# Hybrid decoder block, fp32: the mixer's temporaries move from one pool before the split buffers to two pools around them, and its block orders are searched anew

## Chip, core and metric

One NeuronCore of one Trainium2 chip runs the whole block. The metric is device time in microseconds (us) per execution; the time of a kernel is the median of its runs. Profiled executions are described by a span (first to last instruction), which is a little shorter than the device time of the same execution.

## What is computed

The reference is one decoder layer on 256 tokens of width 2048, in float32, with D_FF = 5632:

```python
x = x + 0.5 * swiglu_ffn(rms_norm(x, ffn1_norm), ffn1_w_gate, ffn1_w_up, ffn1_w_down)
z = rms_norm(x, mix_norm) @ w_in                  # 2048 x 5120: lru_x, lru_gate, sc_b, sc_c, sc_x
xc = causal_depthwise_conv(lru_x, lru_conv_w) + lru_conv_b
h = rg_lru(xc, lru_w_a, lru_b_a, lru_w_i, lru_b_i, lru_lambda)
y_lru = h * gelu(lru_gate)
y_sc = sc_b * causal_depthwise_conv(sc_c * sc_x, sc_conv_w)
y = concatenate([rms_norm(y_lru, lru_out_norm), rms_norm(y_sc, sc_out_norm)])
x = x + y @ w_out                                 # 2048 x 2048
x = x + 0.5 * swiglu_ffn(rms_norm(x, ffn2_norm), ffn2_w_gate, ffn2_w_up, ffn2_w_down)
out = rms_norm(x, final_norm)
```

## The kernel before

**Arithmetic.** TensorE (PE) multiplies in fp32r, which keeps fewer bits than float32. Every operand is therefore kept as two fp32r tiles: `hi`, the value rounded, and `lo`, the rest. A weight tile arrives by DMA as `raw` (128 x 4 x 512 f32, 1 MB), ScalarE (ACT) casts it to `hi` in two halves (CAST 128x1024), VectorE (DVE) subtracts (`lo = raw - hi`, TENSOR_TENSOR 128x2048), and PE forms hi*hi, hi*lo and lo*hi. A set of such a weight tile is called a unit. In a PE row `out<-a,b`, a is the moving operand (512 columns, or 256) and b the stationary one (128 columns). In most blocks the weights move; in the plain blocks `in_x` and `in_b` the weights are stationary and the normalised input `xT_nm` moves.

**Blocks.** Large products are done in blocks by a seven-product scheme in the manner of Strassen and Winograd (`sevens`, line 542): units `p0` to `p6` are seven products of weight quarters or of their sums (12 matmuls of 512 columns each), and units such as `x00` or `x11` are ordinary products for the rest of the inner dimension (24 matmuls each). ACT and DVE put the results together in PSUM and in temporaries. An order such as `"c": ["-", "p0", "p4", "x01", ...]` says in which order PE does the units of a block; `X0`, `X1`, `g2`, `g3` are short fillers: two sets of transposes of the product of conv inputs (`pt_c`), and gate matmuls (`pgate`).

**Stages.** FFN1 runs to about 694 us; the mixer (`mix`, line 1713) to about 945 us: plain block `in_x` (x of the LRU), blocks `c`, `x`, `g` (each a call of `sevens`), plain block `in_b`, and the first output column `o0`; then `lead` (line 2326): output column `o3`, the block `o_q`, and the start of FFN2, which runs to the end.

**The order of work** is not decided at run time. `Plan` (line 57) is a list scheduler in the kernel's own source: each step has an engine, a length, needs, and perhaps a list of `rooms` (buffers) of which it takes the one that comes free first, by the plan's own clock. The steps are written out in the order that it finds, so each engine's queue is a fixed list. SyncE (SP) issues the loads in order, and an issue that waits for its buffer holds up all later ones. A wait that the plan didn't foresee is still honoured: the tile framework puts a semaphore wait on any instruction whose bytes are still in use by an earlier one.

**Memory.** Two stacks of pools lie in SBUF (left and right). From the left: constants, ten big blocks (B0 to B9, `bigs`), then in the FFN stages a pool of 11 temporaries of 2048 bytes per partition (22,528 bytes), and behind it three pairs of split buffers, `pair0` to `pair2` (hi 8192 and lo 8192 bytes each); from the right: raw buffers `raw0` to `raw4` and a spare. Layout "three" of `open_stage` (line 331) has three pairs and five raws, layout "two", for the mixer, two pairs and three raws. In the mixer the pool of temporaries, "mix", is 11 tiles `m` of 4160 bytes (4 x 259 f32, since some hold 3 columns of convolution history, rounded up) and 6 tiles `k` of 2048 bytes: 58,048 bytes ahead of the pairs. So pair0 begins at byte 112,224 of a partition in the FFN stages and at byte 147,744 in the mixer; pair1 begins at 128,608 and at 164,128; hi and lo are 8192 bytes apart. Divided by 128 the first of each leaves 96, the second 32; the big blocks leave 96. In blocks x and g the units take pair0, pair1 and a pair of big blocks (B4, B5) in turn (`thirds`); block c, o0 and the plain blocks use the two pairs alone. FFN1's pair2 lies at bytes 144,992 to 161,376, raw3 and raw4 from 165,792 to 182,176.

**Between stages**, `hand_over` (line 368) tells the next plan when each buffer comes free, from the offsets of pairs and raws in the two layouts, both counted from the start of pair0. `lead` starts its plan with it.

The places that the change and the prediction touch: `Place` (line 1670), `mix_orders` (1705), `middle`, `small`, `keep`, `large_one` in `mix` (1713 on), and the first lines of `lead` (2326). Rows of the profile all carry line 42, the helper that records every operation; they are told apart by tile names.

Of the kernel before, what the change touches and what calls it, by code (L numbers as in the profile page):

```python
# [10 lines left out]
F32 = mybir.dt.float32  # L11
F32R = mybir.dt.float32r
# [4 lines left out]
P = 128  # L17
D = 2048
S = 256
# [3 lines left out]
CW = 512  # L23
NC_D = D // CW
UK = 4
NH = 8
# [174 lines left out]
def hybrid_block(ctx: ExitStack, tc: tile.TileContext, a: dict, out: bass.AP):  # L201
# [4 lines left out]
    x = a["x"][0]  # L206
# [3 lines left out]
    bigs = ctx.enter_context(tc.tile_pool(name="bigs", bufs=10, side="left"))  # L210
# [15 lines left out]
    def f32(ap):  # L226
        return ap.bitcast(F32)
# [103 lines left out]
    def open_stage(layout, raws=None):  # L331

        n = len(opened) + 1
        left, right = layouts[layout]
        for side, names in (("left", left), ("right", right)):
            for name in names:
                pools[name] = pool_of(f"{name}_{n}", side, 2 if name == "spare" else 1)
        if raws:
            recent["raw"] = deque(raws)
        recent["pair"] = deque([i for i in recent["pair"] if i < len(left)] + [i for i in range(len(left)) if i not in recent["pair"]])  # L340
        opened.append(layout)
# [11 lines left out]
    for layout, (left, right) in layouts.items():  # L353
        sizes = dict(short0=6, short1=6, tall1=10, tall2=10, kept0=10, kept1=10, spare=4)
        at, span = 0, {}
# [5 lines left out]
        at = 92.375  # L361
# [6 lines left out]
    def hand_over(ready, old, new):  # L368

        out = {}  # L370
        for name, (lo, hi) in spans[new].items():
            times = [ready.get(n, Plan.EARLY) for n, (a, b) in spans[old].items() if a < hi and lo < b]
            out[name] = max(times, default=Plan.EARLY)
        return out
# [153 lines left out]
    def fetch(plan, w, cs, runs, name, rooms):  # L528
        got = {}

        def run(room):
            rows = sum(n for _, n in runs)
            raw = got["raw"] = pools[room].tile([P, rows, CW], F32, tag="raw", name=f"raw_{name}")
            at = 0
            for k, n in runs:
                sp.dma_start(raw[:, at : at + n, :], w[k * P : (k + n) * P, cs].rearrange("(j p) c -> p j c", p=P))
                at += n

        step = plan.load(sum(n for _, n in runs), run, rooms)
        return step, lambda: got["raw"]  # L540
# [407 lines left out]
    def whole(u):  # L948
        return [(UK * u, UK)]

    def quad(tile):
        return tile.rearrange("p (j c) -> p j c", j=UK)
# [692 lines left out]
    n1 = Norm("n1", vec["ffn1_norm"])  # L1645
# [23 lines left out]
    def past_steps(plan, old, steps):  # L1669
        at = max([z.end for z in steps if z.end is not None], default=Plan.EARLY) - old.free["PE"]  # L1670
        return [plan.add("", 0.0, None, *[z for z in steps if z.end is None], at=at)]

    class Place:
# [3 lines left out]

        def first(self, plan, engine, length, fn, *needs, **more):
            def run(room):
                self.tile = self.make()  # L1680
                fn()

            self.owner = plan.add(engine, length, run, *needs, room=self.rooms, **more)
            return self.owner
# [6 lines left out]
        def keep(self):  # L1691
            self.owner.readers.append(Step("", 0.0, None, (), 0.0, None, Plan.EARLY))
# [7 lines left out]
    for name in blocks_of:  # L1700
# [2 lines left out]
    tt_256, tt_512, tt_1024, ts_256 = 0.35, 0.6, 1.17, 0.41  # L1703
    act_256, act_512, act_1024, scaled_256, scaled_512 = 0.33, 0.6, 1.05, 0.43, 0.67
    mix_orders = {
# [4 lines left out]
    }  # L1710
    rs, yT, kept_yv = [], [], []
# [1 line left out]
    def mix(old):  # L1713
        free, ready = old.finish()
        end = old.free["PE"]
        mixer = ExitStack()
        room = mixer.enter_context(tc.tile_pool(name="mix", bufs=1, side="left", reuse_waits="tile"))
        open_stage("two")
        mixer.callback(close_stage)
        plan = Plan(free, hand_over(ready, "three", "two"))  # L1720
        plan.take(old)
        plan.table, plan.patience = "sqrt", 1.0
        raws, mids, smalls = [f"raw{i}" for i in range(3)], [f"m{i}" for i in range(11)], [f"k{i}" for i in range(6)]
        large = [f"B{i}" for i in range(6)]
        thirds = iter([0, 1, "x"] * 20)
        pairs = iter([0, 1] * 60)

        past = lambda steps: past_steps(plan, old, steps)

        def middle(name, w=S, dt=F32, rooms=None):  # L1730
            return Place(rooms or mids, lambda: room.tile([P, UK, w], dt, tag="m", name=name, bufs=len(mids)))

        def small(name):
            return Place(smalls, lambda: room.tile([P, CW], F32, tag="k", name=name, bufs=len(smalls)))

        def keep(name):
            return room.tile([P, CW], F32, tag="k", name=name, bufs=len(smalls))

        def large_one(name, dt=F32R, rooms=None):
            return Place(rooms or large, lambda: bigs.tile([P, UK, 2 * S], dt, tag="big", name=name))  # L1740

        turned = {c: [] for c in range(NC_D)}
        for c in (0, 1):
# [19 lines left out]

        si = Stationaries()
        xis = [large_one(f"xis_{i}", rooms=[f"B{i}"]) for i in range(2)]
        spare = small("spare_i")
        quads = {(t, u): lambda t=t, u=u: nm.exact[:, :, u * S + t * P : u * S + (t + 1) * P] for t in range(NT) for u in range(2)}

        def part_of(i):
            o = S * (i in (5, 2))  # L1770
            x = xis[0 if i in (4, 5) else 1].tile
            return x[:, :, o : o + P], x[:, :, o + P : o + S]

        def operand_sums():
            def spare_quad():
                return quad(spare.tile)

            exact = {(t, u): past(held["turned", u][1]) for t in range(NT) for u in range(2)}
            fills, steps = sums_in_steps(
                plan, si, lambda: nm.xT[0], lambda: nm.xT[1], quads, spare_quad,  # L1780
                {i: (lambda i=i: part_of(i)[0], lambda i=i: part_of(i)[1]) for i in (4, 5, 6, 2)}, exact,
            )
            for place, step in ((spare, steps[0]), (xis[0], fills[4][0]), (xis[1], fills[6][0])):
                place.owner = step
                step.room = place.rooms

                def run(room, place=place, fn=step.fn):
                    place.tile = place.make()
                    fn()

                step.fn = run
            fills[5][0].needs.append(fills[4][0])
            fills[2][0].needs.append(fills[6][0])
            spare.owner.readers += steps
            for x in xis:
                x.keep()
            xv = Step("", 0.0, None, (), 0.0, None, Plan.EARLY)
            xv.readers = list(steps)
            plan.tenant["B5"] = xv
            return fills  # L1800
# [73 lines left out]
        def gate_weights(key, src, place):  # L1874
            got = {}

            def run(room):
                got["raw"] = pools[room].tile([P, NH, P], F32, tag="raw", name=f"rawgate_{key}")
                sp.dma_start(got["raw"], src.rearrange("h i j -> i h j"))

            load = plan.load(2, run, raws)
            both = Place([place], lambda: bigs.tile([P, 2, NH, P], F32R, tag="big", name=f"gate_{key}"))
            wgate[key] = both
            hi = both.first(plan, "ACT", act_1024, lambda: act.copy(both.tile[:, 0], got["raw"]), load)
            lo = both.by(
                plan, "DVE", tt_1024, lambda: dve.tensor_tensor(both.tile[:, 1], got["raw"], f32(both.tile[:, 0]), op=ALU.subtract), hi
            )
            load.readers += [hi, lo]
            gates_known.extend([hi, lo])
# [395 lines left out]
        for g in range(2):  # L2285
# [7 lines left out]
            for k in (2 * g, 2 * g + 1):  # L2293
                load, raw = fetch(plan, w_out, slice(0, CW), whole(k), f"o0_{k}", raws)
# [13 lines left out]
            class Factor:  # L2308
                name = f"y{g}"

            rs.append(Factor())
            known = factor_in_steps(plan, rs[g], [a], n=D // 2, source=lambda got=got: got["ps"][:, :NT], due=6.0)
# [13 lines left out]
    def lead(keep):  # L2326
        old, added, exact = held["mixed"]
        free, ready = old.finish()
        plan = Plan(free, hand_over(ready, "two", "three"))
        plan.patience = 1.0  # L2330
        plan.take(old)
        rooms = [f"raw{i}" for i in range(5)]
# [16 lines left out]
                home["spare"] = quad(keep("yspare"))  # L2349
            return home["spare"]  # L2350

        known = past_steps(plan, old, exact)
        fills, _ = sums_in_steps(
            plan, so, lambda: yT[0].tile, lambda: yT[1].tile, {(t, u): y(t, u) for t in range(NT) for u in range(2)}, spare,
            {i: (lambda i=i: sum_part(i)[0], lambda i=i: sum_part(i)[1]) for i in (4, 5, 6, 2)},
# [20 lines left out]
        for g in range(2):  # L2376
# [7 lines left out]
            for k in (2 * g, 2 * g + 1):  # L2384
                load, raw = fetch(plan, w_out, slice(3 * CW, 4 * CW), whole(k), f"o3_{k}", rooms)
# [31 lines left out]
        return plan, turned, turn, pairs, [last]  # L2417

    held["mixed"] = mix(held["left"])

    fss = const.tile([P, NT, NC_D], F32, name="fss")
# [165 lines left out]
```

## Time and profile before

| | |
|---|---|
| median of 3 runs | 1708.87 us (1708.69 to 1709.17) |
| profiled execution, its own time | 1708.86 us |
| its span | 1707.1 us |
| mean granted TensorE clock | 0.997 |
| instructions | 20060 |
| HBM read | 339.82 MB, 200 GB/s over the span |

A row of the timeline reads: start, length, engine, line, operation, tiles, shape, count, and in brackets the idle time just before it with what ended it. Matmuls overlap by some 0.16 us at their ends, so the difference of two starts, not the length, tells a group's rate. A row of the chain gives start, length and work on the path that ended last, where "SPq" is SyncE issuing and "DMA" a transfer. The table of windows has for each stretch the busy time of each engine, the granted clock and the DMA share.

### The profile page before, as it was taken

How to read it: one execution, taken by the hardware profiler on the slowest of the kernel's cores; microseconds unless marked ns; L12 is line 12 of the kernel's file. 1: busy time of each engine (PE TensorE's matmuls, PEld its weight loads, DVE VectorE, ACT ScalarE, POOL GpSimd, SP SyncE). 2: the span in 40 equal slices, each digit the busy share in tenths (PEclk: the TensorE clock that was granted, in tenths of full speed). 3: DMA queues.
4: the chain of work that ended last, by engine and by line, in shares of the span. 5: the costliest groups of instructions: out<-in, count | busy, mean ns of one | idle time of the engine just before them, and what ended most of it. 6: DMA issues, size and time to landing. Idle time of an engine off the chain costs nothing.

```text
span 1707.1 us, 20060 instructions
## 1 busy us (share of the span) xinstructions
PE 1691.3 (99%) x7733; PEld 1402.9 (82%) x7733; DVE 1549.7 (91%) x1271; ACT 1117.5 (65%) x1303; POOL 68.3 (4%) x90
## 2 busy tenths in 40 slices
PE   9999999999999999999999999999999999999998
PEld 7888888888888888887888788888888888888886
DVE  7999899999899999798899778999899998999997
ACT  6775576666566668587786575665666665667665
POOL 0200000000000000000000000000000000000000
PEclk9999999999999999999999999999999999999999
DMA  8777877768777968487854786777768878868884
GB/s 283 225 258 211 280 230 237 256 187 262 253 258 228 292 180 266 149 264 223 269 170 135 246 255 196 254 244 211 246 188 264 269 222 246 278 217 249 247 249 145
DMA packets 185295, 398.79 MB, mean 234 GB/s; under 512 B 8052, under 2 KB 10992, under 8 KB 178928
## 3 DMA queue, kind: packets, MB, share of 16 engines
q1 hardware_dynamic: 174912, 340.81, 57.0%
q0 software_dynamic: 10112, 55.65, 16.8%
q8 instruction: 60, 0.98, 0.2%
q10 hardware_dynamic: 176, 1.06, 0.2%
q14 instruction: 35, 0.29, 0.0%
HBM read 339.82 MB, written 2.10 MB: 200 GB/s over the span
## 4 chain that ended last, share of the span: by engine, by line
PE 98%; DMA 1%; ACT 1%; DVE 0%; SPq 0%; issue 0%; DVEq 0%; ACTq 0%
PE ps_u_a L42 10%; PE ps_g_a L42 10%; PE ps_d_a L42 9%; PE ps_u_c L42 6%; PE ps_g_c L42 6%; PE ps_d_c L42 5%; PE ps_u_d L42 4%; PE ps_g_d L42 4%; PE ps_d_d L42 4%; PE ps_d_e L42 4%; PE ps_d L42 4%; PE ps_g_e L42 3%; PE ps_in_x L42 3%; PE ps_in_b L42 3%; PE ps_u L42 2%; PE ps_u_e L42 2%
## 5 line engine op out<-in xcount | busy, mean ns | idle before, releaser
L42 ACT CAST hi_g_p<-raw_g_w 128x1024 fp32r<-128x1024 f32 (+1 forms) x140 | 172.6, 1263 | 114.1 <-DVE raw_g_w L42 42.9
L42 ACT CAST hi_u_p<-raw_u_w 128x1024 fp32r<-128x1024 f32 (+1 forms) x140 | 172.5, 1262 | 93.3 <-PE ps_u_a L42 37.5
L42 DVE TENSOR_TENSOR lo_g_p<-raw_g_w,hi_g_p 128x2560 fp32r<-128x2560 f32 (+2 forms) x90 | 199.4, 2228 | 29.9 <-PE ps_d L42 11.4
L42 DVE TENSOR_TENSOR lo_u_p<-raw_u_w,hi_u_p 128x2560 fp32r<-128x2560 f32 (+2 forms) x90 | 199.5, 2229 | 14.7 <-ACT hi_u_p L42 12.4
L42 ACT CAST hi_d_p<-raw_d_w 128x1024 fp32r<-128x1024 f32 x140 | 141.2, 1047 | 78.7 <-DVE raw_d_w L42 39.6
L42 DVE TENSOR_TENSOR lo_d_p<-raw_d_w,hi_d_p 128x2048 fp32r<-128x2048 f32 (+1 forms) x90 | 162.5, 1814 | 11.2 <-ACT hi_d_p L42 9.8
L42 ACT CAST hi_d_x<-raw_d_x 128x1024 fp32r<-128x1024 f32 x72 | 73.2, 1046 | 36.0 <-PE ps_d_c L42 11.9
L42 DVE TENSOR_TENSOR lo_d_x<-raw_d_x,hi_d_x 128x2048 fp32r<-128x2048 f32 x36 | 82.2, 2286 | 6.7 <-ACT hi_d_x L42 6.6
L42 DVE TENSOR_TENSOR raw_g_w<-raw_g_w,raw_g_w 128x1024 f32<-128x1024 f32 (+2 forms) x50 | 86.5, 1755 | 1.4 <-DMA raw_g_w<-in_ffn_w_gate_dram 0.9
L42 DVE TENSOR_TENSOR raw_u_w<-raw_u_w,raw_u_w 128x1024 f32<-128x1024 f32 (+2 forms) x50 | 86.7, 1756 | 0.6
L42 ACT CAST hi_g_x<-raw_g_x 128x1536 fp32r<-128x1536 f32 x40 | 59.1, 1478 | 24.2 <-DMA raw_g_x<-in_ffn_w_gate_dram 16.5
L42 DVE TENSOR_TENSOR lo_u_x<-raw_u_x,hi_u_x 128x1536 fp32r<-128x1536 f32 x40 | 70.1, 1752 | 1.1 <-ACT hi_u_x L42 1.0
L42 DVE TENSOR_TENSOR lo_g_x<-raw_g_x,hi_g_x 128x1536 fp32r<-128x1536 f32 x40 | 70.1, 1752 | 0.4 <-ACT hi_g_x L42 0.4
L42 ACT CAST hi_u_x<-raw_u_x 128x1536 fp32r<-128x1536 f32 x40 | 59.0, 1476 | 15.8 <-DMA raw_u_x<-in_ffn_w_up_dram 8.6
L42 PE MATMUL ps_u_a<-hi_u_p,xT_n 128*128 128x512 f32 x240 | 61.1, 390 | 0.0
L42 PE MATMUL ps_g_a<-hi_g_p,xT_n 128*128 128x512 f32 x240 | 60.9, 389 | 0.0
L42 PEld LDWEIGHTS ps_g_a<-hi_g_p,xT_n 128*128 128x128 f32 x240 | 45.1, 188 | 9.3
L42 PEld LDWEIGHTS ps_u_a<-hi_u_p,xT_n 128*128 128x128 f32 x240 | 44.9, 188 | 9.2
L42 DVE TENSOR_TENSOR raw_d_w<-raw_d_w,raw_d_w 128x1024 f32<-128x1024 f32 x40 | 48.2, 1220 | 0.3
L42 PE MATMUL ps_d<-hi_d,h 128*128 128x512 f32 x192 | 45.7, 390 | 0.0
L42 PEld LDWEIGHTS ps_d<-hi_d,h 128*128 128x128 f32 x192 | 35.9, 188 | 7.4
L42 PE MATMUL ps_d_a<-hi_d_p,h 128*128 128x512 f32 x160 | 40.0, 392 | 0.0
(581 smaller groups left out, 4159.1 us busy)
## 6 DMA issues: line engine op xcount, KB each, us to landing
raw_g_w<-in_ffn_w_gate_dram SPq DMA_DIRECT2D x40, 1024.0 KB, 6.4
raw_u_w<-in_ffn_w_up_dram SPq DMA_DIRECT2D x40, 1024.0 KB, 6.2
raw_d_w<-in_ffn_w_down_dram SPq DMA_DIRECT2D x40, 1024.0 KB, 6.0
raw_d_x<-in_ffn_w_down_dram SPq DMA_DIRECT2D x36, 1024.0 KB, 6.3
raw_g_x<-in_ffn_w_gate_dram SPq DMA_DIRECT2D x40, 768.0 KB, 7.6
raw_u_x<-in_ffn_w_up_dram SPq DMA_DIRECT2D x40, 768.0 KB, 7.0
raw_d_w<-raw_d_w POOLq DMA_DIRECT2D x20, 1024.0 KB, 7.4
raw_d<-in_ffn_w_down_dram SPq DMA_DIRECT2D x12, 1024.0 KB, 8.2
```

What stands on the lines that cost most here:

```text
L42: ins = getattr(self.engine, name)(*args, **kwargs)
```

## The change

The pool "mix" is replaced by two. "near" stands where "mix" stood and holds 2 tiles `n` of 4096 bytes and 7 tiles `k` of 2048 bytes: 22,528 bytes, the same as the feed-forwards' pool of temporaries, so that pair0 and pair1 begin at bytes 112,224 and 128,608 in the mixer too. "far" stands behind the two pairs, from byte 144,992 on: 4 tiles `mp` of 4160 bytes, which alone can hold the convolution's history, and 5 tiles `m` of 4096. There are 11 tiles of the middle size as before, and 7 small ones where there were 6. The orders of blocks c, x and g are new. In `lead`, the buffers hi2, lo2, raw3 and raw4, which lie where "far" lies, are held not to be free before the last of the `m` and `mp` tiles; and one list of steps also waits, in the plan alone, for the last of `n` and `k`. The counts of instructions on each engine stay the same; apart from blocks c, x and g, each engine's order stays the same too, though what its instructions wait for does not.

```diff
     mix_orders = {
-        "c": ["-", "p0", "p4", "x01", "p5", "p2", "p6", "x11", "p3", "p1", "x00", "x10", "g2", "g3"],
-        "x": ["-", "p0", "p1", "p4", "x01", "p2", "p5", "x11", "p6", "x00", "p3", "x10"],
-        "g": ["-", "p0", "p4", "X1", "x11", "x01", "p5", "p1", "p6", "p2", "x00", "x10", "p3", "X0"],
+        "c": ["-", "p0", "p4", "x01", "p5", "p1", "p6", "x11", "p2", "p3", "x00", "x10", "g3", "g2"],
+        "x": ["-", "p0", "p1", "p4", "x01", "p5", "p2", "p6", "x11", "x00", "p3", "x10"],
+        "g": ["-", "p0", "p4", "X0", "x01", "p5", "p1", "X1", "x11", "p6", "p2", "p3", "x10", "x00"],
...
-        room = mixer.enter_context(tc.tile_pool(name="mix", bufs=1, side="left", reuse_waits="tile"))
+        near = mixer.enter_context(tc.tile_pool(name="near", bufs=1, side="left", reuse_waits="tile"))
         open_stage("two")
         mixer.callback(close_stage)
+        far = mixer.enter_context(tc.tile_pool(name="far", bufs=1, side="left", reuse_waits="tile"))
...
-        raws, mids, smalls = [f"raw{i}" for i in range(3)], [f"m{i}" for i in range(11)], [f"k{i}" for i in range(6)]
+        raws, mids, smalls = [f"raw{i}" for i in range(3)], [f"mp{i}" for i in range(4)], [f"k{i}" for i in range(7)]
+        plain = ["n0", "n1"] + [f"m{i}" for i in range(5)] + mids
...
-        def middle(name, w=S, dt=F32, rooms=None):
-            return Place(rooms or mids, lambda: room.tile([P, UK, w], dt, tag="m", name=name, bufs=len(mids)))
+        def middle(name, w=S, dt=F32):
+            def make(room):
+                if room[0] == "n":
+                    return near.tile([P, UK, w], dt, tag="n", name=name, bufs=2)
+                tag = room.rstrip("0123456789")
+                return far.tile([P, UK, w], dt, tag=tag, name=name, bufs=len(mids) if tag == "mp" else 5)
+
+            return Place(plain if w == S else mids, make)
...
     def lead(keep):
         old, added, exact = held["mixed"]
         free, ready = old.finish()
-        plan = Plan(free, hand_over(ready, "two", "three"))
+        after = hand_over(ready, "two", "three")
+        for name in ("hi2", "lo2", "raw3", "raw4"):
+            after[name] = max(t for n, t in ready.items() if n[0] == "m")
+        plan = Plan(free, after)
...
-        known = past_steps(plan, old, exact)
+        exact = past_steps(plan, old, exact)
+        known = [plan.add("", 0.0, None, *exact, at=max(t for n, t in ready.items() if n[0] in "kn"))]
```

What the change moves is shown at three places. First, SyncE's queue at the end of the mixer, where the loads of `o3` (the first work of `lead`) follow those of `o0`. Numbers at the ends of names count tiles; what stands in brackets are the semaphores that an issue waits for, by engine or DMA queue. Before:

```order
L42 DMA raw_o0_2_7254<-in_w_out_dram 128x4x512 [waits DMAHW0_49,DVE_49]
L42 DMA raw_o0_3_7300<-in_w_out_dram 128x4x512 [waits DMAHW1_49,DVE_49]
L42 DMA raw_o3_0_7515<-in_w_out_dram 128x4x512 [waits DVE_49,PE_49]
L42 DMA raw_o3_1_7517<-in_w_out_dram 128x4x512
L42 DMA raw_o3_2_7519<-in_w_out_dram 128x4x512 [waits DMAHW2_49]
L42 DMA raw_o3_3_7521<-in_w_out_dram 128x4x512 [waits DMAHW3_49]
L42 DMA raw_o_q_w11_7525<-in_w_out_dram 128x4x512 [waits DMAHW4_49,DVE_49]
```

And now:

```order
L42 DMA raw_o0_2_7252<-in_w_out_dram 128x4x512 [waits DMAHW0_49,DVE_49]
L42 DMA raw_o0_3_7317<-in_w_out_dram 128x4x512 [waits DMAHW1_49,DVE_49]
L42 DMA raw_o3_0_7519<-in_w_out_dram 128x4x512 [waits DMAHW2_49,DVE_49]
L42 DMA raw_o3_1_7521<-in_w_out_dram 128x4x512 [waits DMAHW3_49,DVE_49]
L42 DMA raw_o3_2_7523<-in_w_out_dram 128x4x512 [waits DVE_49]
L42 DMA raw_o3_3_7525<-in_w_out_dram 128x4x512
L42 DMA raw_o_q_w11_7529<-in_w_out_dram 128x4x512 [waits DMAHW4_49,DVE_49]
```

The order is the same, but the first load of o3 no longer waits for PE. Before, its room was raw3, whose bytes the mixer's pair1 covered, and PE_49 stood for the last product of `o0_2`, which reads pair1's lo. Now it goes to raw1 and waits for DVE's `lo_o0_1`; the second goes to raw0 and waits for `lo_o0_2`; the third and fourth, into raw3 and raw4 where "far" lies, wait for DVE's sum of `ysq_2` and `ysq_3`. Behind the loads, ACT's casts keep their order too: first half of `hi_o3_1`, `hi_o3_0`, second half of `hi_o3_1`; `hi_o3_1` no longer waits for PE, and `hi_o3_0`, in pair1, waits for the hi products of `o0_2`.

Second, ACT's queue where FFN1 ends and the mixer begins; `hi_in_x0_0` is the mixer's first unit. Before:

```order
L42 CAST hi_d1_4_1_x01_5296<-raw_d1_4_1_x01_5242 128x1024 [waits DMAHW6_49,DVE_49,PE_49]
L42 CAST hi_d1_4_1_x01_5296<-raw_d1_4_1_x01_5242 128x1024
L42 ACTIVATE junk_nm_3_0_5338,ss_nm_4712<-xres_70 128x512 [waits DVE_49,Activation_49]
L42 CAST hi_in_x0_0_5407<-raw_in_x0_0_5398 128x1024 [waits DMAHW7_49,PE_49]
L42 CAST hi_in_x0_1_5412<-raw_in_x0_1_5400 128x1024 [waits DMAHW0_49]
L42 CAST xis_0_5417<-spare_i_5404 128x4x128 [waits DVE_49]
```

And now:

```order
L42 CAST hi_d1_4_1_x01_5296<-raw_d1_4_1_x01_5242 128x1024 [waits DMAHW6_49,DVE_49,PE_49]
L42 CAST hi_d1_4_1_x01_5296<-raw_d1_4_1_x01_5242 128x1024
L42 ACTIVATE junk_nm_3_0_5338,ss_nm_4712<-xres_70 128x512 [waits DVE_49,Activation_49]
L42 CAST hi_in_x0_0_5410<-raw_in_x0_0_5401 128x1024 [waits DMAHW7_49,PE_49]
L42 CAST hi_in_x0_1_5415<-raw_in_x0_1_5403 128x1024 [waits DMAHW0_49,PE_49]
L42 CAST xis_0_5420<-spare_i_5407 128x4x128 [waits DVE_49]
```

The order is the same again, and what PE_49 stands for has moved. Before it was the last product of FFN1's last unit, `p3`, in pair2, which the mixer's pair0 overlapped. Now `hi_in_x0_0` takes pair0's own bytes and waits for the hi products of unit `x10`; `hi_in_x0_1` takes pair1's and waits for the hi products of `x01`.

Third, DVE's queue in block c, where the new order puts `p1` in the place of `p2`. Before:

```order
L42 TENSOR_TENSOR lo_in_c_p5_5987<-raw_in_c_w11_5720,hi_in_c_p5_5960 128x1024 x2
L42 SCALAR_TENSOR_TENSOR xc_1_5989<-zx_1_5912,cols_conv_633,xc_1_5989 128x256 x3
L42 TENSOR_TENSOR lo_in_c_p2_6017<-raw_in_c_w22_5800,hi_in_c_p2_5999 128x2048
L42 TENSOR_TENSOR lo_in_c_p6_6038<-raw_in_c_w12_5732,hi_in_c_p6_6023 128x2048
L42 TENSOR_TENSOR lo_in_c_x11_6066<-raw_in_c_x11_5983,hi_in_c_x11_6044 128x2048
L42 TENSOR_TENSOR lo_in_c_p3_6096<-raw_in_c_w11_5720,hi_in_c_p3_6078 128x2048
L42 TENSOR_TENSOR lo_in_c_p1_6122<-raw_in_c_w21_5826,hi_in_c_p1_6107 128x2048
```

And now:

```order
L42 TENSOR_TENSOR lo_in_c_p5_5990<-raw_in_c_w11_5723,hi_in_c_p5_5963 128x1024 x2
L42 SCALAR_TENSOR_TENSOR xc_1_5992<-zx_1_5915,cols_conv_633,xc_1_5992 128x256 x3
L42 TENSOR_TENSOR lo_in_c_p1_6020<-raw_in_c_w21_5829,hi_in_c_p1_6002 128x2048
L42 TENSOR_TENSOR lo_in_c_p6_6039<-raw_in_c_w12_5735,hi_in_c_p6_6026 128x2048
L42 TENSOR_TENSOR lo_in_c_x11_6068<-raw_in_c_x11_5986,hi_in_c_x11_6045 128x2048
L42 TENSOR_TENSOR lo_in_c_p2_6083<-raw_in_c_w22_5803,hi_in_c_p2_6066 128x2048
L42 TENSOR_TENSOR lo_in_c_p3_6125<-raw_in_c_w11_5723,hi_in_c_p3_6107 128x2048
```

A subtraction of the same size stands at each place; `p1` reads `w21` where `p2` read `w22`, and `p2` comes after `x11`.

More of the change, by code (lines that the diff above doesn't have):

```diff
@@ L1679, in run @@
             def run(room):
-                self.tile = self.make()
+                self.tile = self.make(room)
                 fn()
@@ L1728, in mix, with keep @@
         past = lambda steps: past_steps(plan, old, steps)
-        def middle(name, w=S, dt=F32, rooms=None):
-            return Place(rooms or mids, lambda: room.tile([P, UK, w], dt, tag="m", name=name, bufs=len(mids)))
+        def middle(name, w=S, dt=F32):
[5 more added lines that the diff above has]
+            return Place(plain if w == S else mids, make)
+        def keep(name):
+            return near.tile([P, CW], F32, tag="k", name=name, bufs=len(smalls))
         def small(name):
-            return Place(smalls, lambda: room.tile([P, CW], F32, tag="k", name=name, bufs=len(smalls)))
-        def keep(name):
-            return room.tile([P, CW], F32, tag="k", name=name, bufs=len(smalls))
+            return Place(smalls, lambda room: keep(name))
         def large_one(name, dt=F32R, rooms=None):
-            return Place(rooms or large, lambda: bigs.tile([P, UK, 2 * S], dt, tag="big", name=name))
+            return Place(rooms or large, lambda room: bigs.tile([P, UK, 2 * S], dt, tag="big", name=name))
         turned = {c: [] for c in range(NC_D)}
@@ L1787, in run @@
                 def run(room, place=place, fn=step.fn):
-                    place.tile = place.make()
+                    place.tile = place.make(room)
                     fn()
@@ L1881, in gate_weights @@
             load = plan.load(2, run, raws)
-            both = Place([place], lambda: bigs.tile([P, 2, NH, P], F32R, tag="big", name=f"gate_{key}"))
+            both = Place([place], lambda room: bigs.tile([P, 2, NH, P], F32R, tag="big", name=f"gate_{key}"))
             wgate[key] = both
```

## The prediction

> **What bounds the kernel now.** I read the page first: busy time and the chain that ended last.
>
> ```profile
> PE 1691.3 (99%) x7733; PEld 1402.9 (82%) x7733; DVE 1549.7 (91%) x1271; ACT 1117.5 (65%) x1303; POOL 68.3 (4%) x90
> PE 98%; DMA 1%; ACT 1%; DVE 0%; SPq 0%; issue 0%; DVEq 0%; ACTq 0%
> ```
>
> PE is busy for 1691.3 of a span of 1707.1 us and is 98% of the chain. The change takes no matmul away, so only two things can be had: PE's idle time, and time per matmul. PE's waits show the idle time:
>
> ```profile
> PE ps_o L42 <- ACT hi_o L42: 4.0, 1, 4.0
> PE ps_in_x L42 <- ACT hi_in_x L42: 1.1, 1, 1.1
> PE idle L42 <- DVE ones L42: 1.1, 1, 1.1
> PE ps_in_x_d L42 <- ACT ps_in_x_d L42: 0.7, 1, 0.7
> ```
>
> The columns are total, times and longest. The third row is the kernel's start, which the change doesn't reach. The first is the mixer's exit, the second its entry, the fourth lies in block x. So the places to look at are the two seams between stages, where the change moves buffers.
>
> **The exit.** The chain there, and PE's timeline:
>
> ```profile
> 933.21 0.34 PE pst L42 x4
> ...
> 939.28 0.37 SPq L42
> ...
> 939.70 7.39 DMA raw_o<-in_w_out_dram
> ...
> 947.19 2.00 ACT hi_o L42 x2
> ```
>
> ```profile
> 937.22 2.03 PE L42 MATMUL ps_o<-lo_o,yT 128*128 128x512 f32 x8
> ...
> 944.69 0.50 PE L42 MATMUL pst<-ones,acc 128*128 128x1 f32 x4
> 949.24 5.54 PE L42 MATMUL ps_o<-hi_o,yT 128*128 128x512 f32 x16 [4.05 <-ACT hi_o L42]
> ...
> 956.45 3.79 PE L42 MATMUL ps_o<-hi_o,yT 128*128 128x512 f32 x16
> ...
> 961.89 3.79 PE L42 MATMUL ps_o<-hi_o,yT 128*128 128x512 f32 x16
> ```
>
> SyncE could issue the first load of o3 only at 939.28, when the lo products of o0_2 (begun at 937.22) had left pair1. The load that ACT's first cast needs took 7.39, and PE sat idle for 4.05 us. Then the group of 16 took 5.54 instead of 3.79. Without the stall the next start follows pst by 0.34 (the row at 933.21), not by 949.24 - 944.69 = 4.55: 4.21 saved. One o3 unit takes 961.89 - 956.45 = 5.44, and the first took 956.45 - 949.24 = 7.21: 1.77 more. Together **6.0 us**.
>
> Does the change remove all of it, and what is late next? DVE's rows on which the loads will wait:
>
> ```profile
> 922.27 2.29 DVE L42 TENSOR_TENSOR lo_o<-raw_o,hi_o 128x2048 fp32r<-128x2048 f32 x1 [1.71 <-ACT hi_o L42]
> ...
> 928.33 2.28 DVE L42 TENSOR_TENSOR lo_o<-raw_o,hi_o 128x2048 fp32r<-128x2048 f32 x1
> ...
> 931.78 0.69 DVE L42 TENSOR_TENSOR ysq<-ysq 128x512 f32<-128x512 f32 x1
> ...
> 950.16 4.50 DVE L42 TENSOR_TENSOR lo_o<-raw_o,hi_o 128x2048 fp32r<-128x2048 f32 x2 [10.92 <-ACT hi_o L42]
> ```
>
> The first load now waits for lo_o0_1, which ends at 924.6; the second for lo_o0_2, at 930.6; the last two for a sum that is done by 931.8. By a transfer of 7.39 the second lands near 938.4. ACT casts half of hi_o3_1, then hi_o3_0, which also waits for the hi products of o0_2 (over by about 937.4): 938.4 + 1.0 + 2.0 = 941.4, and DVE's lo, at 2.29, is done near 943.7. PE wants hi at 944.69 + 0.34 = 945.0 and lo at 945.0 + 3.6 = 948.7. So 3.6 and 5.0 us are to spare. Behind these four, SyncE holds the loads of o_q, which wait for o3's subtractions; the first of those began at 950.16 and now at 941.4, 8.8 us earlier, while PE comes 6.0 earlier, so they fall behind nobody. I take 6.0; the bounds are 4.2, if the slow group stays, and 6.2.
>
> **The entry.** PE's timeline, then ACT's:
>
> ```profile
> 682.30 1.98 PE L42 MATMUL ps_d_d<-hi_d_x,h 128*128 128x512 f32 x8
> ...
> 687.74 1.98 PE L42 MATMUL ps_d_c<-hi_d_x,h 128*128 128x512 f32 x8
> ...
> 693.18 1.07 PE L42 MATMUL ps_d_a<-lo_d_p,h 128*128 128x512 f32 x4
> 695.38 3.94 PE L42 MATMUL ps_in_x<-xT_nm,hi_in_x 128*128 128x512 f32 x16 [1.13 <-ACT hi_in_x L42]
> ```
>
> ```profile
> 687.45 0.18 ACT L42 ACTIVATION_READ_ACCUMULATOR junk_nm<-xres 128x1 f32 x1
> 694.28 3.89 ACT L42 CAST hi_in_x<-raw_in_x 128x1024 fp32r<-128x1024 f32 x4 [6.65 <-PE ps_d_a L42]
> ```
>
> ACT waited 6.65 us for FFN1's last unit to leave pair2. Now hi_in_x0_0 waits for x10's hi products, over at 682.30 + 1.98 = 684.3, and hi_in_x0_1 for x01's, over at 689.7. ACT is free at 687.6; the first pair of casts is done at 689.6, the second near 691.7, and PE wants them from 694.1 on. The stall goes with over 4 us to spare. It is worth 695.38 - 693.18 = 2.20 less four matmuls of 0.91, which is 1.3, and 0.1 by which that first group is longer than in_b's (3.82, below): **1.4 us**.
>
> **The rate of matmuls.** In blocks c, x and g the chain's pieces, which abut, show two rates for the same shape. In block c, then in g a unit from the pairs and one from the big blocks:
>
> ```profile
> 747.79 2.80 PE ps_in_c_c L42 x12
> ...
> 758.99 2.80 PE ps_in_c_c L42 x12
> ...
> 761.79 2.80 PE ps_in_c_a L42 x12
> ```
>
> ```profile
> 840.77 1.87 PE ps_in_g_c L42 x8
> ...
> 846.34 1.81 PE ps_in_g_c L42 x8
> ```
>
> And FFN1's down projection, and o0, the mixer's last column:
>
> ```profile
> 660.70 2.72 PE ps_d_c L42 x12
> ...
> 691.53 2.73 PE ps_d_a L42 x12
> ```
>
> ```profile
> 922.02 11.19 PE ps_o L42 x48
> ```
>
> 2.80 by 12 and 11.19 by 48 are 233 ns; 2.72 by 12 and 1.81 by 8 are 226.5 ns. Every slow group moves weights from the mixer's pairs; the unit at 846.34 lies in B4 and B5, and FFN1's in its own pairs. The clock isn't it: it was granted in full in block c (1.00, in the row of windows below), and the two units of g are neighbours. The difference is in the address: the slow tiles begin at 32 over a multiple of 128 bytes, the fast ones at 96. It isn't the region of memory, as FFN1's pair2 lies across the mixer's pair0 and is fast (its last unit, 2.73 at 691.53). The change brings pair0 and pair1 to the feed-forwards' addresses. The matmuls concerned are block c's 180 (7 units of 12, 4 of 24), x's 132 and g's 108 outside B4 and B5, and o0's 96: 516 at 2.80/12 - 2.72/12 = 6.7 ns, **3.4 us**.
>
> The Trainium skill speaks against this term: "TensorE: Matmul & The Clock Gate", section "Wait — 56ns, not 53.3ns?", gives a warm matmul N / 2.4 GHz plus about 2.5 ns, 215.7 ns at 512 columns, with nothing for where an operand lies. By it moving the pairs is worth nothing; the trace has neither figure, and two of its own.
>
> In in_x and in_b the weights are stationary:
>
> ```profile
> 897.98 1.98 PE L42 MATMUL ps_in_b<-xT_nm,lo_in_b 128*128 128x256 f32 x16
> 899.79 3.82 PE L42 MATMUL ps_in_b<-xT_nm,hi_in_b 128*128 128x512 f32 x16
> ```
>
> ```profile
> 699.16 2.05 PE L42 MATMUL ps_in_x<-xT_nm,lo_in_x 128*128 128x256 f32 x16
> ```
>
> Against 3.79 at 956.45 a hi group has 0.03 more, and there are 16 of them: 0.5 us, and a little more where a group follows transposes. If it has the same cause, **0.6 us** goes; the bounds are 0 and 0.8. The lo groups of 256 columns took 1.98 or 2.05, both with weights at 32 over a multiple of 128, so I take nothing for them; 16 times the 0.07 between the two bounds it by about 1.0.
>
> **What could be given back.** PE becomes faster, DVE doesn't:
>
> ```profile
> 745.00:787.00 42.00, 42.00 (x182) 33.66 (x182) 38.69 (x39) 33.15 (x47) 1.67 (x2) 1.00 0.84 250
> ```
>
> ```profile
> 757.26 2.29 DVE L42 TENSOR_TENSOR lo_in_c_p<-raw_in_c_w,hi_in_c_p 128x2048 fp32r<-128x2048 f32 x1
> 760.12 2.29 DVE L42 TENSOR_TENSOR lo_in_c_p<-raw_in_c_w,hi_in_c_p 128x2048 fp32r<-128x2048 f32 x1 [0.57 <-ACT hi_in_c_p L42]
> ```
>
> DVE (third of the busy times) works 38.69 of 42.00 us in block c; 180 matmuls at 226.5 ns need 40.8, so it still fits. The tight place is p2 and p6: their lo parts are ready at 759.6 and 762.4, and PE wants each after eight hi products, 1.87 into its piece, at about 760.8 and 763.6: 1.2 us to spare. By then PE has gained 72 matmuls of 6.7 ns, 0.5 us. p1 in p2's place needs a subtraction of the same 2.29. That leaves 0.7, so the new order needn't stall, but a reordered block may do so by a few tenths: 0 to 1.4 for c, x and g together, and I take 0.7. The fourth wait (0.7, a seed between p0 and p1 of x) stays, since these still stand side by side. The rest costs nothing: the seventh small tile and the split into padded and plain tiles issue nothing.
>
> The sum is made on the profiled execution, 1708.86 us of its own time, which is the median to 0.01: 1708.86 - 6.0 - 1.4 - 3.4 - 0.6 + 0.7 = **1698.2 us**.
>
> **The rivals.**
>
> *The address is not the cause* (chance 0.15). Rate and address go together in the trace, but no row shows one tile at both addresses. Against it stands g, where neighbouring units differ by place alone; for it, that the pairs are also the busiest buffers, so that the 6.7 ns could be a clash with ACT and DVE. Then 4.0 us stay: 1702.2, or 1702.8 with all that could be given back. The rule quoted above from the Trainium skill would have it so.
>
> *The exit's stall comes back smaller* (0.08). hi_o3_1 is first in ACT's queue, and its load may land late, say by 7 us in place of the 3.6 to spare; PE would wait 3.4, plus up to the 1.77 of the slow restart: 1701.6 to 1703.4. The 1.13 us wait at the entry was followed by a group of 3.94, so a short wait costs little more than itself. For it: a transfer took 7.39 there. Against: the first two loads now start 6 us apart, so that they don't share the engines, and only the last two start together.
>
> *Slower: DVE becomes the bound of block c* (0.02). Each subtraction that the new order moves ahead of a unit which PE wants costs 2.29, and bites once the 0.7 us are used up. To turn a gain of 11.4 into a loss of 3.4 takes 14.8 us, six or seven subtractions too early. Then the time is 1712.3 or more. Against it: DVE does the same work in c, at the same places but for p1, p2 and p3.
>
> *The change does nothing measurable* (0.03): new waits on "far" hold up the exit as raw3 did, and the address isn't the cause. With 6.0 and 4.0 not had, and 1.4 had, about 1707.5.
>
> **How the numbers follow.** The forecast has a chance of 0.72. Low end: 6.2 + 1.4 + 3.5 + 0.8 + 1.0 with nothing given back, 1696.0. High end: the first rival, 1702.8, which takes in most of the second as well. About 0.2% (3.4 us, to 1705.45) is what a measurement of this kernel can tell from no change. Forecast and the first two rivals are all faster by more: 0.95. Same 0.03, slower 0.02.
>
> **What would show it.** Right, if PE's waits lose the rows ps_o and ps_in_x; the group after pst takes 3.79; SyncE issues the first load of o3 some 20 us before PE's pst (924.6 against 944.69), not 5; and twelve products of block c take 2.72. Wrong, if c keeps 2.80 (then the address is not it), if a wait of ps_o for hi_o remains, or if PE's waits show lo_in_c, lo_in_x or lo_in_g with more than 1.4 in all.

## The result, and the profile after

The changed kernel takes 1698.7 us (median of 4 runs, 1698.42 to 1699.28) against 1709.02 for the kernel before in the same comparison (4 runs, 1708.69 to 1710.1): a ratio of 0.9939, with a 95% interval of 0.9922 to 0.9956. It is faster, by 10.3 us by the medians; the spans of the two profiled executions, 1707.1 and 1697.0 us, differ by 10.1. 1698.2 was predicted.

Busy times and the chain on the page of the kernel after:

```profile
PE 1686.5 (99%) x7733; PEld 1403.1 (83%) x7733; DVE 1550.4 (91%) x1271; ACT 1119.7 (66%) x1303; POOL 68.5 (4%) x90
PE 99%; ACT 0%; DMA 0%; DVE 0%; issue 0%; DVEq 0%; SPq 0%; ACTq 0%
```

The same 7733 matmuls keep PE busy for 4.8 us less, and the steps of DMA and ACT fall from 1% of the chain each to 0%. PE's waits after the change, with the total, the times and the longest of each:

```profile
PE idle L42 <- DVE ones L42: 1.1, 1, 1.1
PE ps_in_x_d L42 <- ACT ps_in_x_d L42: 0.7, 1, 0.7
PE ps_g L42 <- ACT hi_g L42: 0.4, 1, 0.4
```

The rows of ps_o (4.0 us) and ps_in_x (1.1) are gone, and no new one stands in the mixer. At the exit PE's timeline now reads:

```profile
940.45 0.50 PE L42 MATMUL pst<-ones,acc 128*128 128x1 f32 x4
940.81 3.92 PE L42 MATMUL ps_o<-hi_o,yT 128*128 128x512 f32 x16
944.57 1.98 PE L42 MATMUL ps_o<-lo_o,yT 128*128 128x512 f32 x8
```

The first group of o3 follows pst by 0.36 us, not 4.55, and takes 3.92, not 5.54. SyncE's own timeline shows why (the row merges the four issues):

```profile
920.80 8.10 SPq L42 DMA_DIRECT2D raw_o<-in_w_out_dram  x4
```

The first of o3's four loads is issued at 920.80, 19.7 us before pst; before the change it was issued at 939.28, 5.4 before it. At the entry PE runs through, and ACT's casts come early:

```profile
693.36 1.07 PE L42 MATMUL ps_d_a<-lo_d_p,h 128*128 128x512 f32 x4
694.27 3.79 PE L42 MATMUL ps_in_x<-xT_nm,hi_in_x 128*128 128x512 f32 x16
```

```profile
687.73 1.98 ACT L42 CAST hi_in_x<-raw_in_x 128x1024 fp32r<-128x1024 f32 x2
689.94 2.00 ACT L42 CAST hi_in_x<-raw_in_x 128x1024 fp32r<-128x1024 f32 x2 [0.23 <-PE ps_d_c L42]
```

The first unit is ready at 689.7, and the second waits only 0.23 for the hi products of x01 (ps_d_c). In the chain the rate has changed: block c, a unit of g in the pairs and one in the big blocks, and o0:

```profile
746.77 2.72 PE ps_in_c_c L42 x12
...
757.65 2.72 PE ps_in_c_d L42 x12
760.37 2.72 PE ps_in_c_a L42 x12
...
837.59 1.81 PE ps_in_g_c L42 x8
...
849.38 1.81 PE ps_in_g_c L42 x8
...
918.32 10.91 PE ps_o L42 x48
```

Twelve products of c take 2.72 where they took 2.80, and o0's 48 take 10.91 where they took 11.19. In in_b, whose weights are stationary:

```profile
888.41 2.08 PE L42 MATMUL ps_in_b<-xT_nm,lo_in_b 128*128 128x256 f32 x16
890.32 3.82 PE L42 MATMUL ps_in_b<-xT_nm,hi_in_b 128*128 128x512 f32 x16
```

And before:

```profile
892.42 2.05 PE L42 MATMUL ps_in_b<-xT_nm,lo_in_b 128*128 128x256 f32 x16
894.30 3.84 PE L42 MATMUL ps_in_b<-xT_nm,hi_in_b 128*128 128x512 f32 x16
```

The lo groups have become longer. Now all eight of in_b take 1.91 us from start to start (890.32 - 888.41). Before, five of the eight took 1.88 (894.30 - 892.42) and three 1.81 (899.79 - 897.98, shown in the prediction). The groups of after say it for all of in_b (busy time, mean ns of one):

```profile
L42 PE MATMUL ps_in_b<-xT_nm,hi_in_b 128*128 128x512 f32 x128 | 30.7, 392 | 0.0
...
L42 PE MATMUL ps_in_b<-xT_nm,lo_in_b 128*128 128x256 f32 x128 | 16.6, 283 | 0.0
```

Before, the same two groups were busy for 30.9 and 16.2 us.

Where the 10.1 us went, from the starts of each stage's first matmul in PE's timeline:

| stretch | before | after | change |
|---|---|---|---|
| FFN1's last matmul to block c (entry and in_x) | 50.97 | 49.82 | -1.15 |
| block c | 44.83 | 43.64 | -1.19 |
| block x | 42.67 | 41.78 | -0.89 |
| block g | 43.47 | 42.60 | -0.87 |
| in_b | 46.06 | 46.27 | +0.21 |
| o0 | 22.83 | 22.29 | -0.54 |
| pst to o3 | 4.55 | 0.36 | -4.19 |
| o3 | 23.53 | 21.89 | -1.64 |
| o_q to the last matmul | 725.69 | 725.69 | 0.00 |

FFN1's last matmul begins 0.18 later than before, at 694.04 against 693.86; with the same FFN1 it begins at 693.74 in b_counted and at 694.26 in a_uncounted, so that is no effect of the change. The sum is -10.26 + 0.18 = -10.1.

### The profile page after: what moved, and what is told of

It is laid out like the page before. It is cut to its first block, busy times and chain, and to the rows that moved or that the text cites. A ratio compares the mean times of both kernels' runs of the same rounds, so it can differ in the third digit from the quotient of the medians.

```text
span 1697.0 us, 20056 instructions
## 1 busy us (share of the span) xinstructions
PE 1686.5 (99%) x7733; PEld 1403.1 (83%) x7733; DVE 1550.4 (91%) x1271; ACT 1119.7 (66%) x1303; POOL 68.5 (4%) x90
## 4 chain that ended last, share of the span: by engine, by line
PE 99%; ACT 0%; DMA 0%; DVE 0%; issue 0%; DVEq 0%; SPq 0%; ACTq 0%
PE ps_u_a L42 10%; PE ps_g_a L42 10%; PE ps_d_a L42 9%; PE ps_u_c L42 6%; PE ps_g_c L42 6%; PE ps_d_c L42 5%; PE ps_u_d L42 4%; PE ps_g_d L42 4%; PE ps_d_d L42 4%; PE ps_d_e L42 4%; PE ps_d L42 4%; PE ps_g_e L42 3%; PE ps_in_b L42 3%; PE ps_in_x L42 3%; PE ps_o L42 3%; PE ps_u L42 2%
## 5 line engine op out<-in xcount | busy, mean ns | idle before, releaser
L42 DVE TENSOR_TENSOR lo_g_p<-raw_g_w,hi_g_p 128x2560 fp32r<-128x2560 f32 (+2 forms) x90 | 199.4, 2228 | 30.9 <-PE ps_d L42 11.4
```

Source lines behind the costliest of these rows:

```text
L42: ins = getattr(self.engine, name)(*args, **kwargs)
```

## Experiments

The theory of the prediction: two stalls go, and matmuls with weights in the mixer's pairs become faster because the pairs' residue to 128 bytes changes from 32 to 96. Its rivals: the rate is not a matter of addresses; the exit's stall has more than one cause; the new orders have a part in the gain. Medians of the kernel before vary from 1709.0 to 1710.0 between comparisons, so terms under 1 us are read from the stretches of the timeline.

**The addresses alone** (b_mix64). The kernel before, with 64 bytes more in its pool:

```diff
         room = mixer.enter_context(tc.tile_pool(name="mix", bufs=1, side="left", reuse_waits="tile"))
+        room.tile([P, 16], F32, tag="pad", name="pad")
         open_stage("two")
```

> The kernel before with 64 bytes added at the end of the pool mix, so that the mixer's pairs begin at 96 over a multiple of 128 instead of 32; nothing else changes. If the address sets the rate of matmuls with moving weights: twelve products of block c take 2.72 instead of 2.80 us, c, x, g and o0 give 3.4 us, in_x and in_b lose about 0.5 (as they did after the change), both stalls stay, so about 1706.1. If the rate comes from a clash at the pairs and not from the address: 2.80 and 1709.0 as before.

Measured: 1707.13 us, ratio to before 0.9986 (0.9977 to 0.9995). PE's timeline in block c, in in_b and at the exit:

```profile
747.99 1.98 PE L42 MATMUL ps_in_c_c<-hi_in_c_p,xis 128*128 128x512 f32 x8
749.80 1.07 PE L42 MATMUL ps_in_c_c<-lo_in_c_p,xis 128*128 128x512 f32 x4
750.71 1.98 PE L42 MATMUL ps_in_c_e<-hi_in_c_x,xT_nm 128*128 128x512 f32 x8
...
895.66 2.08 PE L42 MATMUL ps_in_b<-xT_nm,lo_in_b 128*128 128x256 f32 x16
...
946.90 6.47 PE L42 MATMUL ps_o<-hi_o,yT 128*128 128x512 f32 x16 [4.26 <-ACT hi_o L42]
953.21 1.98 PE L42 MATMUL ps_o<-lo_o,yT 128*128 128x512 f32 x8
```

Twelve products take 750.71 - 747.99 = 2.72: 64 bytes of padding do what the move did. c, x, g and o0 give 1.19 + 0.92 + 0.62 + 0.54 = 3.27, in_x and in_b lose 0.21 + 0.28. That would be 2.8 in all. But the exit's stall, still there, grew from 5.8 to 6.9 us, which leaves 1.7: the profiled span is 1.5 shorter than before and the median 2.3, where about 1706.1, a gain of 3, was expected. Of the growth 0.9 us is in o3 itself, at a lower granted clock (third number from the end). The rows of windows of the kernel before, then of b_mix64:

```profile
949.00:953.00 4.00, 3.76 (x10) 3.01 (x11) 2.83 (x2) 4.00 (x6) 0.00 (x0) 0.61 1.05 386
```

```profile
945.00:953.00 8.00, 6.10 (x16) 4.87 (x17) 5.14 (x5) 6.35 (x8) 0.00 (x0) 0.57 1.05 382
```

The clock is as low over 8 us as it was over 4; after the change it is 1.00 over 940 to 948. So the slow group behind the stall, for which the prediction gave no cause, goes with the clock that was granted after PE's idle time. The entry's stretch is 51.18 here and 49.82 after the change, at the same residues, so the entry's stall is worth 1.36. No run takes that stall away by itself.

**The exit alone** (b_counted). The kernel before, with `lead` counting what the pairs had covered:

```diff
-        plan = Plan(free, hand_over(ready, "two", "three"))
+        after = hand_over(ready, "two", "three")
+        for name, under in (("raw3", ("hi1", "lo1")), ("raw4", ("lo1",)), ("hi2", ("hi0",)), ("lo2", ("hi0", "lo0"))):
+            after[name] = max([after[name]] + [ready[n] for n in under if n in ready])
+        plan = Plan(free, after)
```

> The kernel before, with one difference: lead counts the buffers that the mixer's pairs covered (raw3, raw4, hi2, lo2) as not free before the mixer's last units are done, so its first loads go to raw0, raw1 and raw2. Addresses, orders and entry stay. If the exit's stall came from the first load's room alone, PE's wait of 4.05 us and the slow group go: 5.8 to 6.0 us, 1703.1. If another late thing stands behind it (the pair buffers under the temporaries, or the casts): part of the wait stays, 1704 to 1708.

Measured: 1703.12 us, ratio 0.9962 (0.9949 to 0.9974). PE's timeline at the exit:

```profile
944.56 0.50 PE L42 MATMUL pst<-ones,acc 128*128 128x1 f32 x4
944.92 3.90 PE L42 MATMUL ps_o<-hi_o,yT 128*128 128x512 f32 x16
```

The stall goes whole (pst to o3 0.36, o3 21.87), and nothing else in the timeline moves. It was the rooms that `lead` gave to o3's loads, and nothing behind them. The run doesn't part the first load's room from the others'.

**Without the counting** (a_uncounted). The kernel after, with `lead` as it was before:

```diff
-        after = hand_over(ready, "two", "three")
-        for name in ("hi2", "lo2", "raw3", "raw4"):
-            after[name] = max(t for n, t in ready.items() if n[0] == "m")
-        plan = Plan(free, after)
+        plan = Plan(free, hand_over(ready, "two", "three"))
```

> The kernel after without the lines in lead that hold hi2, lo2, raw3 and raw4 back, so its first two loads of o3 go to raw3 and raw4, where the temporaries lie, and wait for the sum of ysq. If the place of the pairs already cures the exit: that sum comes some 12 us before PE wants the first o3 unit, so no wait, 1698.7 within 0.5. If it is the counting in lead that cures it: a wait of ps_o for hi_o of 2 to 4 us and a slow group, 1701 to 1704.

Measured: 1698.75 us, ratio 0.9936 (0.9923 to 0.9948), every stretch from in_b to o_q within 0.01 us of the changed kernel's. Either remedy is enough by itself: the right count in the old places, or the new places.

**The orders** (a_oldorders, b_neworders). The kernel after with the old orders of c, x and g, and the kernel before with the new ones; the edit is the first hunk of the change, backwards and forwards.

> The kernel after with the old orders of blocks c, x and g. If the new orders are worth nothing by themselves, as the prediction has it: 1698.7 within 0.5. If they are what kept block c free of stalls when TensorE became faster: up to 1.4 us more, with rows lo_in_c, lo_in_x or lo_in_g among PE's waits.

> The kernel before with the new orders of blocks c, x and g. If the new orders matter only where PE is faster (with the new places the old ones cost 0.7 to 0.8 in block g): 1709.0 within 0.5. If they are worth the same in the old places: 1708.2.

Measured: 1699.48 us (0.9941, 0.9928 to 0.9953) and 1710.67 (1.0003, 0.9994 to 1.0012). The intervals don't tell either from its neighbour; the stretches do. The first loses 0.77 in block g (43.37 against 42.60), with a wait that neither kernel has; the second loses 0.62 in block x (43.29 against 42.67), with another. PE's timeline of the first, then of the second:

```profile
852.56 2.14 PE L42 MATMUL ps_in_g_a<-hi_in_g_p,xis 128*128 128x512 f32 x8 [0.55 <-ACT u_in_g L42]
```

```profile
823.17 2.12 PE L42 MATMUL ps_in_x_a<-hi_in_x_x,xT_nm 128*128 128x512 f32 x8 [0.30 <-ACT u_in_x L42]
```

So neither set of orders is better in itself. Each fits its own layout, and the search saved the move from giving back 0.8 us. The wait was not for lo_in_c or another of the tiles that I had named, but for ACT's `u_in_g`.

**All residues moved** (left32, left64). The kernel after with 32, or with 64 bytes between the constants and the big blocks:

```diff
+    pad = ctx.enter_context(tc.tile_pool(name="pad", bufs=1, side="left"))
+    pad.tile([P, 16], F32, tag="pad", name="pad")
     bigs = ctx.enter_context(tc.tile_pool(name="bigs", bufs=10, side="left"))
```

(8 elements for 32 bytes.)

> The kernel after with 32 bytes put between the constants and the big blocks, so that all big blocks, temporaries and pairs begin at a multiple of 128 bytes instead of 96 over one; the spare and raw buffers stay. If the residue to 128 sets the rate: another rate than 226.7 ns for 512 columns, and as aligned operands shouldn't be worse, between 0 and 11 ns less (215.7 ns at best), so 1633 to 1699, most likely some ns, 1670 to 1690. If the address is not the cause: 1698.7.

> The kernel after with 64 bytes put there, so that both kinds of operand begin at 32 over a multiple of 128 nearly everywhere. If the address sets the rate: some 5900 matmuls of 512 columns with moving weights at 233.3 ns instead of 226.7, about 39 us more, 1738, or more still if the stationary operand's address adds to it. If the address is not the cause: 1698.7.

Measured: 1698.25 us (0.9934, 0.9921 to 0.9946) and 1697.49 (0.9929, 0.9917 to 0.9942). Neither came out at the 1670 to 1690 and the 1738 us that were expected as likeliest if the residue sets the rate, and here the prediction's theory of the rate fell. With left64 both operands begin at 32 over a multiple of 128, and no stretch is more than 0.01 us longer than after the change; the chain in block c:

```profile
745.89 2.72 PE ps_in_c_c L42 x12
```

Residues of 32, 0 and 96 are all fast as long as both operands have the same. And left64 made something faster, the down projection's matmuls whose stationary operand `hs` lies in the spare pool on the right stack, which the padding doesn't move. PE's timeline of FFN2 after the change, then with left64:

```profile
1608.32 2.03 PE L42 MATMUL ps_d_e<-hi_d_p,hs 128*128 128x512 f32 x8
1610.19 1.10 PE L42 MATMUL ps_d_e<-lo_d_p,hs 128*128 128x512 f32 x4
```

```profile
1606.94 1.98 PE L42 MATMUL ps_d_e<-hi_d_p,hs 128*128 128x512 f32 x8
1608.76 1.07 PE L42 MATMUL ps_d_e<-lo_d_p,hs 128*128 128x512 f32 x4
```

Eight take 1610.19 - 1608.32 = 1.87, against 1.82. The new theory: the rate depends on the difference of the two operands' addresses.

**The difference alone** (sweep). Its loop, with nothing else running on the core:

```diff
+    for columns, name in ((CW, "wide"), (S, "half")):
+        for i in range(16):
+            group(f"{name}_{chr(97 + i)}", columns, 4 * i, 0)
+    for i in range(8):
+        group(f"still_{chr(97 + i)}", CW, 0, 8 * i)
```

> Matmuls alone: it leaves the whole computation out and writes x to the output. Groups of 24 matmuls, each with its own stationary operand, as in the kernel. The stationary operand stays at a multiple of 128 bytes while the moving one begins 0, 16, 32 ... 240 bytes further on (groups a to p), wide with 512 columns and half with 256; then the moving one stays and the stationary one begins 0, 32 ... 224 bytes further on (groups a to h of still). If the rate depends on the difference of the two addresses, with a period of 128 or 256 bytes: wide a takes 226.8 ns, wide e (64 bytes) about 233, still c (64 bytes) about 233, and half a 119.5, half e 116.5. If it depends on the moving operand alone: still stays at 226.8 throughout. If it comes from traffic of other engines and not from the addresses: all wide groups take the same.

The chain of the sweep, each piece 24 matmuls (letters count 16 bytes for wide and half, 32 for still):

```profile
26.38 5.44 PE ps_wide_a L42 x24
...
48.57 5.51 PE ps_wide_e L42 x24
...
70.77 5.59 PE ps_wide_i L42 x24
...
93.17 5.59 PE ps_wide_m L42 x24
...
109.98 5.45 PE ps_wide_p L42 x24
115.42 2.87 PE ps_half_a L42 x24
...
126.79 2.83 PE ps_half_e L42 x24
...
135.38 2.72 PE ps_half_h L42 x24
...
149.46 2.73 PE ps_half_m L42 x24
...
160.71 5.50 PE ps_still_a L42 x24
...
171.80 5.60 PE ps_still_c L42 x24
...
194.21 5.51 PE ps_still_g L42 x24
```

With 512 columns the difference of 0 (a) costs 5.44 / 24 = 226.7 ns and that of -16 (p) 227; every other one costs more, up to 234.6, and so does 128 (i: 233), so the period isn't 128 bytes. That 256 changes nothing is seen in b_mix64, whose pairs begin 140,032 = 547 x 256 bytes after the first big block and are fast. Moving the stationary operand by 64 (still c) costs the same as moving the other by 192 (wide m), and by 192 (still g) the same as the other by 64 (wide e): it is the difference, moving minus stationary. About 233 was expected for still c and for wide e; still c came out so, and e took 229.6, since the kernel before has a difference of 192 and not of 64 to 256.

With 256 columns it is nearly the other way round: 0 is among the costliest differences (119.6), and 112 (h) and 192 (m) are the cheapest (113.3 and 113.8).

The difference is not the whole of it, though. Still a has the addresses of wide a and took 229 ns on average: behind the groups of 256 columns its first ten matmuls took 224 to 236 from start to start, and only the rest 226 to 227. And in the kernel before, with a difference of 64 throughout, in_b's lo groups ran at two rates, 113.3 and 117.8 ns. What chooses between them is not known.

A clash with other engines is excluded here, as none runs.

**Back to the kernel** (a_near64). The kernel after, with the pairs 64 bytes further:

```diff
+        near.tile([P, 16], F32, tag="pad", name="pad")
         open_stage("two")
         mixer.callback(close_stage)
         far = mixer.enter_context(tc.tile_pool(name="far", bufs=1, side="left", reuse_waits="tile"))
```

> The kernel after with 64 bytes added at the end of the pool near: in the mixer the pairs begin 64 bytes further than the big blocks, to 256. Before, they began 192 further, to 256. By the sweep, where the difference moving minus stationary to 256 bytes decides: blocks c, x, g and o0 (difference 64) take 228.9 ns, twelve products 2.75 us, against 2.72 after and 2.80 before; in in_x and in_b (difference 192) the hi groups take 233.5 ns, 3.74 us from start to start, and the lo groups 113.3 ns, 1.81 us. If only the difference to 128 decides: as before, 2.80, 3.68 and 1.87. The pairs now reach 64 bytes into their neighbours' old places, so a wait at the entry or the exit may come back; it is read from the groups' rates.

The chain in block c, and PE's timeline in in_b:

```profile
747.20 2.75 PE ps_in_c_c L42 x12
```

```profile
897.71 3.89 PE L42 MATMUL ps_in_b<-xT_nm,hi_in_b 128*128 128x512 f32 x16
901.43 1.98 PE L42 MATMUL ps_in_b<-xT_nm,lo_in_b 128*128 128x256 f32 x16
903.25 3.89 PE L42 MATMUL ps_in_b<-xT_nm,hi_in_b 128*128 128x512 f32 x16
```

2.75, 3.72 (901.43 - 897.71) and 1.82 (903.25 - 901.43), where 2.75, 3.74 and 1.81 were expected from the sweep; one of in_b's eight lo groups, at 890.26, took 1.89 here. The one execution took 1703.27 us, with two waits of PE that the changed kernel doesn't have: 0.80 for hi_o at the exit and 1.33 for ps_o_q_d in o_q. That they come from the overlap is likely and not shown.

The fastest version run is left64, at 1697.49 us. Its interval overlaps that of the changed kernel; the stretch from o_q to the last matmul, 725.01 against 725.69, shows part of its gain.

## Why the prediction was right

- **The exit**: 6.0 predicted, 4.19 + 1.64 = 5.83 measured. The step held as written: the first load waits for lo_o0_1, nothing takes the stall's place, and b_counted gets the same from the rooms alone. The first group takes 3.92, though, where 3.79 was predicted.
- **The entry**: 1.4 predicted, 1.36 measured (b_mix64 against after, a difference of two kernels and not an edit of its own).
- **The rate of moving weights**: 3.4 predicted, 3.49 measured in c, x, g and o0. The size was right and the cause as stated wrong. That 32 over a multiple of 128 bytes costs more than 96 was true of the rows, but left64 is fast at 32 throughout. What counts for 512 columns is moving minus stationary to 256 bytes: 192 before, 0 after. The count of 516 and the price of 6.7 ns don't depend on which it is, so the term came out. It also hangs on the new orders: with the old ones g keeps only 0.10 of its 0.87 (a_oldorders).
- **Stationary weights**: 0.6 gained was predicted, with a lower bound of 0; 0.21 in in_x and 0.21 in in_b were lost. This step failed. "If it has the same cause" was right, but I priced the groups of 512 columns and took nothing for those of 256. In in_b the hi groups gained 0.2 us together (30.9 to 30.7) and the lo groups lost 0.4 (16.2 to 16.6): each lo matmul now takes 119.4 ns (1.91 / 16), the slow end for 256 columns in the sweep. A bound below 0 was owed there. Nor did the 0.03 by which a hi group's length exceeds 3.79 go: it is 3.82 still, at 890.32.
- **What is given back**: 0.7 taken, 0 measured. DVE kept ahead of PE in block c. Its timeline there, after the change:

```profile
756.15 2.29 DVE L42 TENSOR_TENSOR lo_in_c_p<-raw_in_c_w,hi_in_c_p 128x2048 fp32r<-128x2048 f32 x1
```

  p1's lo ends at 758.4, and PE wants it after eight hi products, at about 757.65 + 1.81 - 0.16 = 759.3. With the old orders 0.77 would have gone, in g and not in c. The errors of the two small terms, 1.0 and 0.7, nearly cancel; that the forecast came within 0.5 us of the result is luck to that extent.
- **The rivals**: that the address is not the cause was wrong: b_mix64 gets 3.27 us from 64 bytes. The rival's second form, a clash with ACT and DVE at busy buffers, fell in the sweep, where neither runs. The rule of the Trainium skill ("TensorE: Matmul & The Clock Gate", "Wait — 56ns, not 53.3ns?") gives 215.7 ns for a warm matmul of 512 columns, with no term for place; the sweep doesn't agree, with 226.7 to 234.6 ns by place alone. These matmuls are fp32r, and no run here shows another type. The exit's stall did not come back, and DVE did not become the bound. (The upper end of the range, 1702.2 with the 0.7 not gained either, adds to 1702.9 and not 1702.8.)

Why the difference of two addresses should set the rate, and why the best differs between 256 and 512 columns, stays open: no run here separates the weight load from the matmul.

## What to carry to other kernels

Buffers that changed their address between stages cost twice here: their first user waited for whatever lay there, and a planner that counted offsets from the wrong origin sent loads into rooms that weren't free. So look at the seams between stages. Where PE is saturated, take the rate of each group from start to start and compare groups of one shape; here 3% in one stage was a matter of where two pools begin relative to each other, and 64 bytes of padding cured it. Orders that were searched for one layout should be searched again for the next, since either set here cost 0.6 to 0.8 us in the other's layout.

## What the runs showed of the hardware

For fp32r matmuls with a new stationary operand each time, the time from start to start varies with the moving minus the stationary address, to 256 bytes. In the sweep, with 512 columns, it is 226.7 ns at 0, 229.6 at 64 and 233 at 192; with 256 columns 119.6 at 0, 117.9 at 64 and 113.8 at 192. In the kernel, block c's twelve products take 2.80 us at 192 (before), 2.75 at 64 (a_near64) and 2.72 at 0 (after).

With 256 columns one difference can show two rates: 113.3 and 117.8 ns at 64 (in_b of before), 113.6 to 114.4 and once 117.8 at 192 (in_b of a_near64).

The cost of a restart is not fixed, and it goes with the granted clock. After 4.05 us of idle (before) o3's first sixteen matmuls took 5.38 from start to start, at a clock of 0.61 over 949 to 953 us; after 4.26 (b_mix64) they took 6.31, at 0.57 over 945 to 953. 3.63 is usual. After 1.13 at the entry sixteen took 3.78.
